# Four pairwise additions in an index lookup, and a denser schedule of gathered rows in the expert stage

## The chip, the cores and the metric

The kernel runs on one core of one Trainium2 chip. The metric is the time of one execution on the device, in microseconds (us). The times below are medians of several executions; the profile is one more execution, recorded by the hardware profiler.

## What is computed

Two layers of a backbone over 256 latent tokens and 256 context tokens, both of width 1024. Each layer has a token mixer (attention, Fourier mixing, pooling, gates) and then an expert network that the reference calls PEER. The change lies in PEER:

```python
def _peer(h, w_pq, peer_keys, peer_down, peer_up):
    q = (h @ w_pq).reshape(B, L, PEER_HEADS, 2, PEER_QDIM // 2)
    s = jnp.einsum("blhpd,hpkd->blhpk", q, peer_keys)
    sv, si = lax.top_k(s, PEER_TOPK)
    cand = (sv[..., 0, :, None] + sv[..., 1, None, :]).reshape(B, L, PEER_HEADS, PEER_TOPK * PEER_TOPK)
    cidx = (si[..., 0, :, None] * N_KEYS + si[..., 1, None, :]).reshape(...)
    top_s, pos = lax.top_k(cand, PEER_TOPK)
    eidx = jnp.take_along_axis(cidx, pos, axis=-1)
    gate = jax.nn.softmax(top_s, axis=-1)
    ...
        a = jnp.einsum("tkd,td->tk", peer_down[ee], hh)
        act = (gg * jax.nn.gelu(a)).astype(hh.dtype)
        return jnp.einsum("tk,tkd->td", act, peer_up[ee])
```

There are 8 heads, 128 keys, 16 picks per head, and so 128 experts for each token out of 16384. The context tokens go through PEER in layer 0 alone; layer 1 has only the 256 latent tokens.

## The kernel before

**Two ways through PEER.** For most tokens the kernel computes all 16384 experts densely: 128 groups of 128 experts, each group multiplied with the weights on TensorE, and the result multiplied by a dense table of gates, G, that is zero where an expert was not picked. In layer 0 this covers 384 of 512 tokens (`ND`). The other 128 tokens (`NS`), one per partition, are done by gathers: for each of the 128 picks GpSimd (POOL) gathers one row of 1024 numbers per token from `down`, VectorE (DVE) forms its dot product with the token's input (L706), and later POOL gathers the row of `up` and DVE adds it, scaled, to an accumulator (L713). That makes 256 such steps, each with one gather of 512 KB; the text calls them *rows*. `rows` is a generator of 256 steps and an end. It keeps two gathers ahead and has three buffers, `gx`. DVE and POOL take their instructions in program order. Each row's DVE instruction is put behind the last weight split that was written before it (`issue_after(self.last)`).

**The expert stage of layer 0** is `experts_both` and `experts`, L767 to L821. Step i of 128 loads the `up` weights of group i, splits them into a high and a low part (ACT writes `wh` at L81, DVE `wl` at L82), does 18 matmuls into `acc` (L789 to L791), and prepares the activations of group i + 4 (`dn`). For the first 60 groups (`EARLY0`) the hidden values were computed earlier, and are loaded from `E` into `ge` (L743); for the others they are computed in the step by 24 more matmuls from `in_downT`. At each step's end `next(pace)` runs the generator of rows at a rate of `ROWS_S` per step for the first 56 steps and `ROWS_N` for the other 72. Every sixth step also advances the modulation of layer 1 (`extra`, weights `in_wmod`). When the 128 steps are through, the sums are transposed (L817) and added to the state (L820), and then `drain(rows)` in `run` writes all rows that are left. After it come a step of modulation and the norm of the latent tokens for layer 1 (`norm`, L215 to L288), whose result the next projections (`latents`, matmuls L91 to L93) need. The sum of the rows is added to the context tokens' state in `rows_out` (L720, L721).

```python
pace = paced(rows, lambda: ROWS_S if done[0] < E.shape[0] else ROWS_N)
def step(i):
    done[0] = i + 4
    next(pace)
    if i % 6 == 5:
        next(extra, None)
```

Rows are also run before the stage: one after each of 16 weight columns in `front` and some beside the scores.

**The index lookup** is the end of `topk`, L602 to L616. For each pick a one-hot mask over 16 candidates is made in bf16 (L607), multiplied with the key numbers (L612), and summed over the 16 candidates by a reduction that walks the candidates with a stride of 16 elements (L614). Each works on 128x1024 elements, half of the heads and one of two key sets at a time: four passes a call. `topk` is called six times, so there are 24 of each. Two calls are woven into the attention of layer 0's latent tokens (`early_routes`), two are in `routes` of layer 0 and two in `routes` of layer 1, beside the building of the gate table (`gates`, L644 to L670) and the hidden values computed early.

The order on each engine is settled when the kernel is built: a scheduler orders the instructions of the program text by when they become ready, and each engine then keeps that order.

Of the kernel before, what the change touches and what calls it, by code (L numbers as in the profile page):

```python
# [16 lines left out]
OP = mybir.AluOpType  # L17
AX = mybir.AxisListType
# [8 lines left out]
WINDOWS = (2, 4, 8, 16)  # L27
TG = 16
EARLY0, EARLY1 = 60, 88
ROWS_O, ROWS_A, ROWS_S, ROWS_N = 1, 0.5, 0.4, 2.6  # L30
SC0, SC1, R0, R1 = 0.5, 0.5, (0.36, 0.46, 0.34), (0.53, 0.9, 0.66)
FILL = (0, 3, 6)
PARTS = ((1, 3), (2, 5), (4,))
# [6 lines left out]
class Net:  # L40
# [520 lines left out]
    def topk(self, sv, si, out):  # L561
        nc, kp = self.nc, self.k
        ts = kp.tile([128, 8, 16], F32, name="tsc", bufs=1)
        pos = kp.tile([128, 128], U32, name="pos", bufs=1)


        for h4 in range(2):
            cd = self.f2([128, 4, 112])
            ra, rb = sv[:, 8 * h4:8 * h4 + 8:2, :], sv[:, 8 * h4 + 1:8 * h4 + 8:2, :]
            nc.vector.tensor_tensor(cd[:, :, 0:64].rearrange("p h (a b) -> p h a b", a=4),  # L570
                                    ra[:, :, 0:4].unsqueeze(3).to_broadcast([128, 4, 4, 16]),
                                    rb.unsqueeze(2).to_broadcast([128, 4, 4, 16]), op=OP.add)
            nc.vector.tensor_tensor(cd[:, :, 64:112].rearrange("p h (a b) -> p h a b", a=12),
                                    ra[:, :, 4:16].unsqueeze(3).to_broadcast([128, 4, 12, 4]),
                                    rb[:, :, 0:4].unsqueeze(2).to_broadcast([128, 4, 12, 4]), op=OP.add)
            for i in range(4):
                hd = 4 * h4 + i
                scr = self.f1([128, 112])
                yield from self.top16(ts[:, hd, :], pos[:, hd * 16:(hd + 1) * 16], cd[:, i, :], scr)
                yield  # L580

        sb = kp.tile([128, 2, 128, 2], BF, name="sb", bufs=1)
        for d in range(2):
            nc.vector.tensor_copy(sb.rearrange("p w (h a) d -> p w h a d", h=8)[:, :, :, :, d],
                                  si.rearrange("p (h w) a -> p w h a", w=2))
        g = kp.tile([128, 8, 16], F32, name="gate", bufs=1)
        sm = kp.tile([128, 8, 2], F32, name="gsum", bufs=1)
        nc.vector.tensor_sub(g, ts, ts[:, :, 0:1].to_broadcast([128, 8, 16]))
        nc.scalar.activation(g, g, AF.Exp)
        nc.vector.reduce_sum(sm[:, :, 0], g, axis=AX.X)  # L590
        nc.vector.reciprocal(sm[:, :, 1], sm[:, :, 0])
        nc.vector.tensor_mul(g, g, sm[:, :, 1:2].to_broadcast([128, 8, 16]))
        pu = self.f2([128, 4, 128], U32)
        nc.vector.tensor_scalar(pu[:, 0, :], pos, 4, None, op0=OP.logical_shift_right)
        nc.vector.tensor_scalar(pu[:, 1, :], pos, 2, None, op0=OP.logical_shift_right)
        nc.vector.tensor_scalar(pu[:, 2, :], pos, 15, None, op0=OP.bitwise_and)
        nc.vector.tensor_scalar(pu[:, 3, :], pos, 3, None, op0=OP.bitwise_and)
        pb = kp.tile([128, 2, 128], BF, name="pb", bufs=1)
        nc.vector.scalar_tensor_tensor(pb[:, 0, :], pu[:, 1, :], -12.0, pu[:, 0, :], op0=OP.add, op1=OP.max)
        nc.vector.scalar_tensor_tensor(pb[:, 1, :], pu[:, 0, :], 4.0, pu[:, 2, :], op0=OP.is_lt, op1=OP.mult)  # L600
        nc.vector.tensor_tensor(pb[:, 1, :], pb[:, 1, :], pu[:, 3, :], op=OP.max)
        ij = kp.tile([128, 2, 128], F32, name="ij", bufs=1)  # L602
        for w in range(2):
            for h4 in range(2):
                ks = slice(64 * h4, 64 * h4 + 64)
                oh = self.f2([128, 4, 16, 16], BF)
                nc.vector.tensor_tensor(  # L607
                    oh, self.iota16.unsqueeze(1).to_broadcast([128, 4, 16, 16]),
                    pb[:, w, ks].rearrange("p (h k) -> p h k", h=4).unsqueeze(2).to_broadcast([128, 4, 16, 16]),
                    op=OP.is_equal)  # L610
                o4 = oh.rearrange("p h a (k d) -> p (h a) k d", d=2)
                nc.vector.tensor_tensor(o4, o4, sb[:, w, ks, :].unsqueeze(2).to_broadcast([128, 64, 8, 2]), op=OP.mult)  # L612
                yield
                nc.vector.reduce_sum(ij[:, w, ks].rearrange("p (h k) -> p h k", h=4),  # L614
                                     oh.rearrange("p h a k -> p h k a"), axis=AX.X)
                yield  # L616
        out += [ij, g]

# [490 lines left out]
```

## Time and profile before

| | us |
|---|---|
| median of 3 executions | 3106.73 |
| lowest and highest | 3104.70 to 3107.01 |
| profiled execution, its own time | 3093.76 |
| its span, first to last instruction | 3092.0 |
| TensorE busy (PE) | 2896.5 (94%) |
| VectorE busy (DVE) | 2341.6 (76%) |
| ScalarE busy (ACT) | 1443.6 (47%) |
| GpSimd busy (POOL) | 322.3 (10%) |
| mean granted TensorE clock | 0.964 |

The profiled execution lies 0.4% under the median of the timed ones. [...] A row of waits names who waited for whom. A matmul that is queued counts as busy, so a busy PE can still be held up by a little.

### The profile page before, as it was taken

What the parts mean: (1) busy time and instruction counts of PE and PEld (TensorE: products, weight loads), DVE (VectorE), ACT (ScalarE), POOL (GpSimd) and SP (SyncE); (2) the same over time, 40 slices, a digit from 0 to 9 for tenths busy, and PEclk for the clock granted to TensorE, in tenths of its full rate; (3) what the DMA queues carried; (4) which work ended last, traced back from release to release, by engine and by line L of the source; (5) the groups of instructions that cost most, each with busy time, mean ns of one, the idle gap of its engine ahead of it and who ended that gap; (6) DMA issues with size and microseconds to landing.
All of it is one profiled execution on the core that took longest, in us unless ns stands there. A gap on an engine that the chain in (4) does not pass through costs nothing.

```text
span 3092.0 us, 53067 instructions
## 1 busy us (share of the span) xinstructions
PE 2896.5 (94%) x18335; PEld 2597.3 (84%) x18335; DVE 2341.6 (76%) x5278; ACT 1443.6 (47%) x2820; POOL 322.3 (10%) x260
## 2 busy tenths in 40 slices
PE   7999899798999999999999996699999999999998
PEld 5799878798999777799998995589889998788997
DVE  6677779889988566688787887755799886676666
ACT  5565444443444333344433332354545555555554
POOL 0000000121000011134333344000000000000000
PEclk8999999999999999999999997799999999999999
DMA  7574443676666877799898987543657778888664
GB/s 249 171 233 144 139 129 116 213 249 199 199 221 213 289 251 263 248 309 327 314 320 308 319 294 264 177 152 123 186 159 228 242 235 283 296 267 286 203 201 141
DMA packets 413519, 708.36 MB, mean 229 GB/s; under 512 B 38336, under 2 KB 160960, under 8 KB 409152
## 3 DMA queue, kind: packets, MB, share of 16 engines
q1 hardware_dynamic: 376384, 570.73, 56.4%
q0 software_dynamic: 36864, 134.23, 13.2%
q8 instruction: 143, 2.34, 0.3%
q14 instruction: 128, 1.05, 0.1%
HBM read 638.49 MB, written 66.32 MB: 228 GB/s over the span
## 4 chain that ended last, share of the span: by engine, by line
PE 43%; DMA 10%; DVE 7%; issue 3%; POOL 1%; ACT 1%; DVEq 0%; SPq 0%; ACTq 0%; POOLq 0%
PE acc L790 6%; PE mm L91 6%; PE acc L791 6%; PE mm L92 6%; PE acc L789 6%; PE mm L93 6%; DMA gx<-in_up,eidx 3%; DMA ge<-E 3%; DVE wl L82 2%; DMA raw<-in_up 1%; DMA gx<-in_down,eidx 1%; PE acc L662 1%; PE acc L91 1%; PE acc L92 1%; PE acc L93 1%
## 5 line engine op out<-in xcount | busy, mean ns | idle before, releaser
L81 ACT CAST wh<-raw 128x512 fp32r<-128x512 f32 x1604 | 973.7, 618 | 834.1 <-PE mm L93 196.3
L82 DVE TENSOR_TENSOR wl<-raw,wh 128x512 fp32r<-128x512 f32 x1604 | 1079.8, 689 | 278.7 <-ACT wh L81 269.3
L91 PE MATMUL mm<-hH,wh 128*128 128x256 f32 (+1 forms) x2432 | 755.6, 311 | 12.8 <-ACT ge L731 8.0
L92 PE MATMUL mm<-hH,wl 128*128 128x256 f32 (+1 forms) x2432 | 748.9, 308 | 12.5 <-DVE wl L82 12.5
L93 PE MATMUL mm<-hL,wh 128*128 128x256 f32 (+1 forms) x2432 | 746.2, 307 | 0.0
L790 PE MATMUL acc<-wl,f 128*128 128x512 f32 x1280 | 506.6, 396 | 16.8 <-DVE wl L82 15.7
L789 PE MATMUL acc<-wh,f 128*128 128x512 f32 x1280 | 502.9, 393 | 5.0 <-ACT f L754 5.0
L791 PE MATMUL acc<-wh,f 128*128 128x512 f32 x1280 | 502.3, 392 | 0.0
L92 PEld LDWEIGHTS mm<-hH,wl 128*128 128x128 f32 x2432 | 467.2, 192 | 19.5 <-DVE wl L82 15.0
L91 PEld LDWEIGHTS mm<-hH,wh 128*128 128x128 f32 x2432 | 466.8, 192 | 18.9 <-ACT ge L731 9.1
L93 PEld LDWEIGHTS mm<-hL,wh 128*128 128x128 f32 x2432 | 466.2, 192 | 0.1
L790 PEld LDWEIGHTS acc<-wl,f 128*128 128x128 f32 x1280 | 242.1, 189 | 77.4 <-DVE wl L82 30.4
L693 POOL DMA_INDIRECT gx<-in_down,eidx x128 | 169.7, 1326 | 1295.5 <-DVE f L713 566.0
L789 PEld LDWEIGHTS acc<-wh,f 128*128 128x128 f32 x1280 | 242.3, 189 | 53.4 <-ACT f L754 5.3
L791 PEld LDWEIGHTS acc<-wh,f 128*128 128x128 f32 x1280 | 242.0, 189 | 49.9
L752 DVE TENSOR_TENSOR ge<-ge,f 128x256 f32<-128x256 f32 (+1 forms) x384 | 136.5, 380 | 180.5 <-DMA ge<-E 147.9
L754 ACT CAST f<-ge 128x384 fp32r<-128x384 f32 (+1 forms) x256 | 117.1, 459 | 284.3 <-DVE ge L752 278.2
L731 ACT ACTIVATE ge<-mm 128x384 f32<-128x384 f32 (+1 forms) x256 | 112.0, 438 | 222.2 <-PE mm L93 215.3
L91 PE MATMUL acc<-hH,wh 128*128 128x256 f32 x688 | 210.2, 306 | 2.0 <-ACT hH L285 2.0
L713 DVE SCALAR_TENSOR_TENSOR f<-gx,av,f 128x1024 f32<-128x1024 f32 x128 | 164.0, 1282 | 56.8 <-DMA gx<-in_up,eidx 56.4
L706 DVE CUSTOM_DVE_ANT_0 gx<-gx,f 128x1024 f32<-128x1024 f32 x128 | 156.3, 1221 | 60.4 <-DMA gx<-in_down,eidx 60.2
L92 PE MATMUL acc<-hH,wl 128*128 128x256 f32 x688 | 199.2, 290 | 0.9 <-DVE wl L82 0.9
(221 smaller groups left out, 3840.8 us busy)
## 6 DMA issues: line engine op xcount, KB each, us to landing
raw<-in_downT SPq DMA_DIRECT2D x512, 256.0 KB, 4.0
raw<-in_up SPq DMA_DIRECT2D x512, 256.0 KB, 4.3
raw<-in_wmod SPq DMA_DIRECT2D x192, 256.0 KB, 3.8
raw<-in_winc SPq DMA_DIRECT2D x172, 256.0 KB, 3.1
G<-f SPq DMA_DIRECT2D x40, 1024.0 KB, 6.0
f<-G SPq DMA_DIRECT2D x32, 1024.0 KB, 7.2
raw<-in_wpq SPq DMA_DIRECT2D x96, 256.0 KB, 3.4
raw<-in_wo SPq DMA_DIRECT2D x48, 256.0 KB, 2.6
```

The lines of the kernel that those rows point to most:

```text
L81: nc.scalar.copy(H, r)
L82: self.last = nc.vector.tensor_sub(L, r, H.bitcast(F32)).ins
L91: t.matmul(out, lhsT=wH, rhs=xH, start=first, stop=False)
L92: t.matmul(out, lhsT=wL, rhs=xH, start=False, stop=False)
L93: t.matmul(out, lhsT=wH, rhs=xL, start=False, stop=last)
L693: nc.gpsimd.indirect_dma_start(out=r, out_offset=None, in_=self.h["up"][0] if up else self.h["down0"], in_offset=bass.IndirectOffsetOnAxis ...
L706: nc.vector.tensor_tensor_reduce(r, r, hot[:, 0, :], op0=OP.mult, op1=OP.add, scale=1.0, scalar=0.0, accum_out=av[:, k:k + 1])
L713: nc.vector.scalar_tensor_tensor(hot[:, 1, :], r, av[:, k:k + 1], hot[:, 1, :], op0=OP.mult, op1=OP.add)
L752: nc.vector.tensor_mul(y, y, Gg[:, :, c, :])
L789: m(p[t][half], lhsT=aH[:, a], rhs=H[:, 0], start=(i == 0), stop=False)
L790: m(p[t][half], lhsT=aH[:, a], rhs=L[:, 0], start=False, stop=False)
L791: m(p[t][half], lhsT=aL[:, a], rhs=H[:, 0], start=False, stop=(i == 127))
```

## The change

Two edits. The rates of rows in the expert stage of layer 0 go from 0.4 and 2.6 to 0.75 and 2.75 per step. The strided reduction of the lookup becomes four additions: eight candidates to eight, four to four, two to two in place in bf16, and the last two into `ij` in fp32. One of the 16 candidates is not zero, so the sums are exact.

```diff
-ROWS_O, ROWS_A, ROWS_S, ROWS_N = 1, 0.5, 0.4, 2.6
+ROWS_O, ROWS_A, ROWS_S, ROWS_N = 1, 0.5, 0.75, 2.75
...
-                nc.vector.reduce_sum(ij[:, w, ks].rearrange("p (h k) -> p h k", h=4),
-                                     oh.rearrange("p h a k -> p h k a"), axis=AX.X)
+
+                for n in (8, 4, 2):
+                    nc.vector.tensor_tensor(oh[:, :, 0:n], oh[:, :, 0:n], oh[:, :, n:2 * n], op=OP.add)
+                nc.vector.tensor_tensor(ij[:, w, ks].rearrange("p (h k) -> p h k", h=4), oh[:, :, 0], oh[:, :, 1],
+                                        op=OP.add)
```

The lines behind the lookup move down by three in the changed kernel: the dot products of rows are L709 there, the additions of rows L716, the state's update L823.

On DVE, at the end of layer 0's expert stage, stood before (`gx` is a gathered row, `wl` a weight split, `xT` the state, `rs` the norm's statistics):

```order
L713 SCALAR_TENSOR_TENSOR f_3782<-gx,av,f_3782 128x1024
L82 TENSOR_TENSOR wl<-raw,wh 128x512
L706 ISA gx,av<-gx,f_3782 128x1024
L175 MEMSET f_21222 128x512
L820 SCALAR_TENSOR_TENSOR xT<-acc,mods_93,xT 128x128 x24
L713 SCALAR_TENSOR_TENSOR f_3782<-gx,av,f_3782 128x1024
L706 ISA gx,av<-gx,f_3782 128x1024
L713 SCALAR_TENSOR_TENSOR f_3782<-gx,av,f_3782 128x1024
L176 CAST f_21222<-sc_87 128x16x4
```

Rows stand on both sides of the state's update and go on between the steps of the norm. The same place in the changed kernel:

```order
L716 SCALAR_TENSOR_TENSOR f_3782<-gx,av,f_3782 128x1024
L755 TENSOR_TENSOR ge<-ge,f_20432 128x256
L755 TENSOR_TENSOR ge<-ge,f_20434 128x128
L82 TENSOR_TENSOR wl<-raw,wh 128x512
L758 TENSOR_TENSOR f_21064<-ge,f_21063 128x384
L82 TENSOR_TENSOR wl<-raw,wh 128x512 x6
L175 MEMSET f_21270 128x512
L823 SCALAR_TENSOR_TENSOR xT<-acc,mods_93,xT 128x128 x24
L176 CAST f_21270<-sc_87 128x16x4
L175 MEMSET f_21271 128x512
```

The last row (L716, first line) now stands ahead of the last group's activations (L758), and none behind it.

On DVE, in the lookup of layer 1's first 128 tokens, stood before (`f_25959` and the like are the masks, `ij` the summed indices):

```order
L614 TENSOR_REDUCE ij<-f_25915 128x64
L607 TENSOR_TENSOR f_25959<-iota16b,pb 128x1024
L82 TENSOR_TENSOR wl<-raw,wh 128x512
L612 TENSOR_TENSOR f_25959<-f_25959,sb 128x1024
L614 TENSOR_REDUCE ij<-f_25959 128x64
```

Each pass is a mask, a product and a reduction, with weight splits between them. The same place in the changed kernel:

```order
L616 TENSOR_TENSOR f_25963<-f_25963 128x4x128
L607 TENSOR_TENSOR f_26010<-iota16b,pb 128x1024
L616 TENSOR_TENSOR f_25963<-f_25963 128x4x64
L612 TENSOR_TENSOR f_26010<-f_26010,sb 128x1024
L616 TENSOR_TENSOR f_25963<-f_25963 128x4x32
L82 TENSOR_TENSOR wl<-raw,wh 128x512
L617 TENSOR_TENSOR ij<-f_25963 128x64
```

The additions of one pass stand between the mask, the product and the weight splits of the next.

## Rows read from the trace of the kernel before

**Rows 1.** Windows: stretch, us, PE, PEld, DVE, ACT, POOL busy, clock, DMA, GB/s.

```profile
1020.00:1291.00 271.00, 255.26 (x1064) 202.85 (x1065) 170.31 (x347) 104.66 (x195) 29.34 (x23) 0.96 0.77 260
1291.00:1886.00 595.00, 590.86 (x2970) 534.27 (x2968) 476.82 (x794) 232.03 (x446) 229.57 (x186) 1.00 0.90 311
1886.00:1958.00 72.00, 27.54 (x95) 19.56 (x94) 52.87 (x103) 17.33 (x35) 27.59 (x23) 0.57 0.69 232
```

**Rows 2.** Windows of L713 alone (rows of up): DVE busy, count in brackets.

```profile
1020.00:1291.00 271.00, 15.50 (x13) 0.96 0.77 260
1291.00:1886.00 595.00, 118.50 (x93) 1.00 0.90 311
1886.00:1958.00 72.00, 21.09 (x17) 0.57 0.69 232
```

**Rows 3.** Windows of L706 alone (rows of down, two instructions each).

```profile
1020.00:1291.00 271.00, 14.75 (x24) 0.96 0.77 260
1291.00:1886.00 595.00, 113.10 (x184) 1.00 0.90 311
1886.00:1958.00 72.00, 9.85 (x16) 0.57 0.69 232
```

**Rows 4.** Timeline of PE behind the expert stage: start us, us, what, [idle before].

```profile
1889.82 0.66 PE L817 MATMUL acc<-ident,f 128*128 128x128 f32 x4 [0.35 <-ACT f L814]
1904.96 0.80 PE L185 MATMUL acc<-wh,f 128*128 128x512 f32 x1 [14.48 <-DVE f L176]
...
1957.19 0.58 PE L91 MATMUL acc<-hH,wh 128*128 128x256 f32 x1 [0.76 <-ACT hH L285]
```

**Rows 5.** Timeline of DVE, same place.

```profile
1895.07 6.17 DVE L820 SCALAR_TENSOR_TENSOR xT<-acc,mods,xT 128x128 f32<-128x128 f32 x24
...
1904.68 0.22 DVE L176 CAST f<-sc 128x64 fp32r<-128x64 f32 x1
...
1914.11 0.16 DVE L225 TENSOR_SCALAR rs<-mm 128x2 f32<-128x2 f32 x1 [2.08 <-PE mm L221]
...
1915.40 0.69 DVE L82 TENSOR_TENSOR wl<-raw,wh 128x512 fp32r<-128x512 f32 x1
...
1954.56 1.28 DVE L271 TENSOR_TENSOR f<-xT,mm 128x512 f32<-128x512 f32 x2
```

**Rows 6.** Waits of DVE from 1886 to 1958, the longest: us in total, times, longest.

```profile
DVE f L713 <- DMA gx<-in_up,eidx: 9.5, 8, 2.1
```

**Rows 7.** Chain that ended last, from 1067 to 1291, shares by line.

```profile
by line: DMA ge<-E 31.0%; DMA raw<-in_up 13.2%; DVE wl L82 11.5%; PE acc L790 8.0%; PE acc L791 7.2%; PE acc L789 6.9%; DVE f L755 6.7%; issue 5.6%; DVE ge L752 2.8%; DMA f<-G 2.1%; DVE gx L706 1.6%; DVE f L713 1.2%; ACT wh L81 0.8%; DVEq L
```

**Rows 8.** Waits of DVE from 1020 to 1291, the longest.

```profile
DVE ge L752 <- DMA ge<-E: 89.8, 38, 4.7
```

**Rows 9.** Waits of DVE from 1291 to 1886, the two longest.

```profile
DVE gx L706 <- DMA gx<-in_down,eidx: 49.6, 35, 4.3
DVE f L713 <- DMA gx<-in_up,eidx: 47.2, 33, 3.7
```

**Rows 10.** The gathers (L693) from 1291 to 1886, from issue to landing.

```profile
DMA to landing us min/median/max: 4.3/6.3/10.0
```

**Rows 11.** DVE groups over the whole span: busy us, mean ns | idle before.

```profile
L656 DVE TENSOR_TENSOR a<-f,gT 128x1536 bf16<-128x1536 bf16 x160 | 148.7, 961 | 5.8 <-PE acc L662 5.8
L652 DVE TENSOR_TENSOR f<-iotab,ijT 128x1024 bf16<-128x1024 bf16 x160 | 106.9, 693 | 0.0
L614 DVE TENSOR_REDUCE ij<-f 128x64 f32<-128x1024 bf16 x24 | 50.7, 2111 | 0.0
```

**Rows 12.** Waits of PE in layer 1's lookups: 2322 to 2342, then 2430 to 2448.

```profile
PE mm L92 <- DVE wl L82: 2.7, 3, 1.3
...
PE acc L662 <- DVE a L656: 3.8, 1, 3.8
```

**Rows 13.** Windows around the lookups of both layers, columns as in the first group.

```profile
440.00:560.00 120.00, 115.70 (x850) 104.49 (x849) 110.51 (x302) 53.86 (x112) 0.00 (x0) 1.00 0.38 117
2290.00:2350.00 60.00, 50.44 (x405) 49.09 (x404) 59.93 (x220) 27.54 (x53) 0.00 (x0) 0.94 0.53 169
```

## The prediction

> **What bounds the kernel now.** I read the windows by stage first, then the timeline around the dip that they show, then the waits and the chain on both sides of it. The expert stage of layer 0 has three parts [rows 1]. In the first (steps 0 to 55, 1020 to 1291 us) PE is busy 255.3 of 271 us, the DMA engines are busy 0.77 and move 260 GB/s; the chain runs mostly through loads of stored hidden values (`ge<-E`, 31%) and of `up` weights (13.2%) [rows 7]. In the second (steps 56 to 127, to 1886) PE is busy 590.9 of 595 us at full clock: it is the bound. [...] DVE takes its work in order, so the state's update, the norm's small steps and the weight splits all wait behind rows that wait for their gathers [rows 6].
>
> **The rows, counted.** The first part takes 56 x 0.4 = 22 rows, the second 72 x 2.6 = 187, and some 24 are left for the third part; the windows show 25 there [rows 2, 3]. With the new rates the two parts ask for 56 x 0.75 = 42 and 72 x 2.75 = 198, that is 20 and 11 more, 31 in all. That covers the 24, so the rows end some two steps before the stage does. The order of the changed kernel says the same: the last row stands ahead of the last group's activations, and none behind the state's update.
>
> **What the third part is worth.** Without rows, the way from the last expert matmul to the first projection is this. The transposes end near 1890.5 [rows 4]; the state's update, 6.17 us, follows them closely and ends near 1894 instead of 1901. From the cast that feeds PE (1904.68) to the norm's first small step (1914.11) it takes 9.4 us now [rows 5]; kept whole, that puts the small steps at 1904. Between them and the diagonal matrices stand nine weight splits of 0.69 us [rows 5] and some eleven small operations, about 8 us: 1912. Diagonals, broadcast and the first part of the normalization need some 4 us more (the last step, from L271 at 1954.56 to the matmul at 1957.19, takes 2.6 [rows 4, 5]): 1916. The splits come from a chain of loads, casts and matmuls at the lower clock that may hold them, so I take 1920. **Gain: 1957 - 1920 = 37 us**, between 30 (the splits wait some 0.8 us each) and 42.
>
> **What the 20 rows cost in the first part.** Below: nothing, if they fall into the time in which DVE waits for `ge`, 89.8 us in 38 waits [rows 8]; a gain is not to be had from more work here. Above: each lies open on DVE with its 1.25 us (15.50 us for 13 additions, 14.75 us for 12 dot products [rows 2, 3]), 25 us. Between these I go by the chain: rows hold 2.8% of the 224 us from 1067 to 1291 [rows 7], 6.3 us for the 21 or so rows there, 0.3 us each. **Cost: 20 x 0.3 = 6, with a little for the transfers 7 us.** Their bytes: 20 x 0.52 MB = 10.5 MB on top of 271 us x 260 GB/s = 70.5 MB, so 299 GB/s if the time stays. The second part moves 311 GB/s with gathers among it [rows 1], so this fits.
>
> **What the 11 rows cost in the second part.** 14 us of DVE work, against 118 us in which DVE is idle, 97 of them waiting for gathers to land [rows 1, 9]. PE has its weights in time there, and three more rows in twenty steps change that little. **Cost: 2 us**, between 0 and the 14.
>
> **What the additions bring.** From 1024 to 1536 elements a bf16 operation of this kind goes from 693 to 961 ns [rows 11]: 0.52 ns an element and 157 ns fixed. The additions of 512, 256 and 128 elements are then 425, 291 and 224 ns, and the last, 64 elements with an fp32 output, at twice the slope also 224: 1.16 us instead of 2.11 us. If all ran at twice the slope it would be 1.63 us. So each of 24 passes gains 0.95 us (at least 0.48), 23 us of DVE in all. What of this is on the path is bounded by what PE waits: where layer 1's lookups stand, DVE is full (59.93 of 60 us) and PE idle for 9.6 [rows 13]; of that, waits of 2.7 us fall among the first four reductions and one of 3.8 us behind the next three [rows 12]. The first vanish, of the last three passes give back 2, and in layer 0, where PE is busy 115.7 of 120 us around the first eight passes [rows 13], I count 1. **Gain: 5 us**, between 2 and 9.
>
> [...] In this trace four operations pay the fixed 157 ns four times, 0.63 us of the 1.16 [rows 11]. [...]
>
> **The sum.** -37 + 7 + 2 - 5 = -33 us. Against the profiled execution's own 3093.8 us this gives 3060.8; it lies 13 us under the median, so the same sum from the median, 3106.7, gives **3074 us**, with an own range of 3057 (all terms at their good ends) to 3097 (two of the four at their bad ends, not all).
>
> **Rivals.**
>
> *No change: the first part pays for the bytes.* If the first part is bound by what the DMA engines bring at its own 260 GB/s, 10.5 MB cost 40 us instead of 7, and the sum is 0: 3107. For it: the chain is 46% loads there [rows 7]. Against it: DMA is busy only 0.77, and 311 GB/s are moved later [rows 1].
>
> *Slower: the first part pays for bytes and DVE one after the other.* A row's gather delays the `ge` load, DVE then waits for `ge`, and the row's own 1.25 us comes on top since DVE keeps its order: 2.0 + 1.25 us a row, 65 us for 20. The sum is -37 + 65 + 2 - 5 = +25: 3132. It decides from 2.0 us a row, where the 40 us of gains net of the second part are eaten. Against it: none of the longest waits of DVE there is for a gather [rows 8], and a row costs the chain 0.3 us now.
>
> *The gathers don't keep up in the second part.* The new rate asks for a row every 595/198 = 3.0 us. Now it is 595/185 = 3.2 us [rows 2, 3]. With three buffers a row's gather (6.3 us at the median from issue to landing [rows 10]) and its 1.25 us on DVE give a pitch of at least 2.5 us; the room is what DVE's order may add. If the pitch stays at 3.2, DVE waits at gathers while weight splits queue behind it, and 198 rows take 634 us instead of 595, less the two steps' room of some 16: +22 instead of +2, 3094. [...]
>
> *The change doesn't do what it says.* The rows were to lag behind their places so far that some are still left at the stage's end, say six at 2.9 us (72 us for 25 rows [rows 2, 3]): 17 us of the 37 stay, 3091. Against it: the order on DVE is fixed, and it has no row behind the update.
>
> **How the numbers follow.** A difference under 0.2% (6 us) can't be told from no change. Forecast 0.73, bytes 0.11, bytes and DVE 0.07, gathers 0.06, rows left 0.03. Faster are the forecast, the gathers and the rows left, 0.82, less 0.01 for the forecast's far tail: 0.81. Same is 0.12, slower 0.07. The range goes from the forecast's lower end, 3057, to 3104: it takes in the two milder rivals and stops short of the bytes and the slower case, which with the tails hold 0.2.
>
> **What would show it.** Behind the stage, no row (L709, L716) after the state's update; the projections' first matmul about 34 us after the last expert matmul instead of 71. The first part 271 us long before and some 278 after, with waits for `ge` no longer than 95 us in total; the second part 597, PE still full. The new operations L616 and L617 at about 425, 291, 224 and 224 ns, and PE's wait of 2.7 us among layer 1's first lookups gone. Wrong would be a first part longer by 25 us or more, PE's busy share in the second part below 98%, or a wait that takes the place of the drained rows, such as splits that wait for the modulation's weights.

## The result, and the profile after

The changed kernel takes **3054.5 us** at the median of four runs (3049.3 to 3060.4); the kernel before 3105.7 at the median of four (3092.9 to 3107.0). The ratio estimated from these runs is 0.985, with an interval of 0.982 to 0.988: faster by 1.5%, some 46 us, where 33 were predicted. The two medians lie 51 us apart; but beside the later experiments the kernel before had medians of 3095.9 to 3098.4 us (11 to 23 executions each), so the gain is nearer to 46. Applied to the 3106.7 us that the forecast started from, the ratio gives 3060 us; the median itself lies 2.5 us under the low end of the range. The profiled execution of after took 3055.25 us (span 3053.5), that of before 3093.8, so the two traces differ by 38.5 us and not by the whole distance of the medians; the rest stands in no trace.

The windows of after, of the three parts of layer 0's expert stage, answer to [rows 1], columns as there (clock is the granted TensorE clock as a share of full speed, DMA the busy share of the DMA engines, GB/s what they moved). Records of matmuls overlap (the last expert matmuls, L792 to L794 from 1892.81 us, have 0.39 us each and start 0.23 us apart), so PE can count as busy while one is queued.

```profile
1010.00:1283.00 273.00, 254.96 (x1066) 204.90 (x1067) 191.16 (x373) 105.21 (x196) 62.86 (x42) 0.96 0.84 290
1283.00:1895.00 612.00, 598.42 (x2968) 535.16 (x2967) 484.85 (x803) 229.27 (x450) 230.08 (x188) 0.99 0.90 309
1895.00:1926.00 31.00, 22.58 (x98) 19.01 (x96) 20.98 (x64) 14.32 (x29) 0.00 (x0) 0.73 0.33 105
```

The first part is 2 us longer, though its DMA engines now move 290 GB/s instead of 260; the second is 17 us longer, which was not foreseen; the third is 41 us shorter and has no gather (POOL x0). The boundaries here are whole us; in the comparisons below the parts are cut at the starts of instructions, as the table has them (us, from the two traces; the first 272 us, ahead of the table, differ by 1 us):

| stretch | before | after | difference |
|---|---|---|---|
| layer 0's first output projection to the end of its second, with the first lookups in between ("early") | 321.1 | 308.5 | -12.6 |
| routes of layer 0 | 427.9 | 430.8 | +2.9 |
| expert stage, steps 0 to 55 | 270.2 | 272.5 | +2.3 |
| expert stage, steps 56 to 127 | 594.1 | 611.7 | +17.6 |
| last expert matmul to first projection of layer 1 | 71.7 | 29.9 | -41.8 |
| projections and attention of layer 1 | 362.7 | 365.7 | +3.0 |
| layer 1's first mask to its expert stage | 286.6 | 279.9 | -6.7 |
| from there to the end | 485.6 | 483.3 | -2.3 |

Behind the stage, the timeline of PE in after (start us, us, what, [idle before]; against [rows 4]):

```profile
1895.08 2.79 PE L820 MATMUL acc<-ident,f 128*128 128x128 f32 x24
...
1902.17 0.78 PE L185 MATMUL acc<-wh,f 128*128 128x512 f32 x1 [4.30 <-DVE f L176]
...
1907.44 3.83 PE L221 MATMUL mm<-ones,f 128*128 128x1 f32 x18
...
1924.56 0.58 PE L91 MATMUL acc<-hH,wh 128*128 128x256 f32 x1 [0.76 <-ACT hH L285]
```

The timeline of DVE in the same place (against [rows 5]):

```profile
1895.72 6.29 DVE L823 SCALAR_TENSOR_TENSOR xT<-acc,mods,xT 128x128 f32<-128x128 f32 x24 [2.22 <-PE acc L820]
...
1911.31 0.16 DVE L225 TENSOR_SCALAR rs<-mm 128x2 f32<-128x2 f32 x1 [7.41 <-PE mm L221]
...
1917.26 0.69 DVE L82 TENSOR_TENSOR wl<-raw,wh 128x512 fp32r<-128x512 f32 x1 [1.75 <-ACT wh L81]
...
1920.73 2.48 DVE L271 TENSOR_TENSOR f<-xT,mm 128x512 f32<-128x512 f32 x4
```

No row stands in it. Work that was late behind rows is now late behind PE: DVE sits idle for 7.41 us until the norm's sums (L221) are there, and these run at a low granted clock: it is 0.51 from 1902 to 1911 us, behind 4.30 us in which PE stood idle, and 0.73 at the mean of the third part (0.57 before). Of the nine splits among the small steps one waits for its cast, 1.75 us.

In the second part the waits of DVE in after (us in total, times, longest us; against [rows 9]):

```profile
DVE gx L709 <- DMA gx<-in_down,eidx: 61.3, 36, 4.5
DVE f L716 <- DMA gx<-in_up,eidx: 53.5, 35, 3.4
```

They grew from 97 to 115 us, and PE's waits there grew with them. Of before:

```profile
PE acc L790 <- DVE wl L82: 2.7, 3, 2.0
PE mm L186 <- DVE wl L82: 1.4, 1, 1.4
```

and of after, where PE waits for the same weight splits 16 times and for activations twice:

```profile
PE acc L793 <- DVE wl L82: 6.1, 12, 1.9
PE mm L91 <- ACT ge L734: 3.8, 2, 3.2
PE mm L186 <- DVE wl L82: 3.6, 4, 1.2
```

The additions in after, as groups over the span (busy us, mean ns | idle before; they take the place of L614 in [rows 11]):

```profile
L616 DVE TENSOR_TENSOR f<-f 128x512 bf16<-128x512 bf16 x24 | 10.0, 417 | 0.0
L616 DVE TENSOR_TENSOR f<-f 128x256 bf16<-128x256 bf16 x24 | 6.8, 284 | 0.0
L616 DVE TENSOR_TENSOR f<-f 128x128 bf16<-128x128 bf16 x24 | 5.2, 218 | 0.0
L617 DVE TENSOR_TENSOR ij<-f 128x64 f32<-128x64 bf16 x24 | 5.2, 216 | 0.1
```

Together 1.135 us a pass instead of 2.111.

### The profile page after: what moved, and what is told of

It is laid out like the page before. It is cut to its first block, busy times and chain, and to the rows that moved or that the text cites. A ratio compares the mean times of both kernels' runs of the same rounds, so it can differ in the third digit from the quotient of the medians.

```text
span 3053.5 us, 53130 instructions
## 1 busy us (share of the span) xinstructions
PE 2895.9 (95%) x18335; PEld 2599.7 (85%) x18335; DVE 2310.3 (76%) x5350; ACT 1438.3 (47%) x2820; POOL 327.4 (11%) x260
## 4 chain that ended last, share of the span: by engine, by line
PE 56%; DVE 18%; DMA 16%; issue 7%; ACT 2%; POOL 1%; DVEq 0%; SPq 0%; ACTq 0%; POOLq 0%
PE mm L91 7%; PE mm L92 7%; PE mm L93 7%; PE acc L793 5%; PE acc L792 5%; PE acc L794 5%; DVE wl L82 4%; DMA ge<-E 4%; DMA gx<-in_up,eidx 4%; PE acc L91 3%; PE acc L93 3%; PE acc L92 3%; DMA gx<-in_down,eidx 3%; DVE a L659 2%; PE acc L665 2%
## 5 line engine op out<-in xcount | busy, mean ns | idle before, releaser
L792 PE MATMUL acc<-wh,f 128*128 128x512 f32 x1280 | 505.0, 394 | 5.0 <-ACT f L757 5.0
L794 PE MATMUL acc<-wh,f 128*128 128x512 f32 x1280 | 503.8, 394 | 0.0
L696 POOL DMA_INDIRECT gx<-in_down,eidx x128 | 178.2, 1392 | 1225.5 <-DVE f L504 553.4
L792 PEld LDWEIGHTS acc<-wh,f 128*128 128x128 f32 x1280 | 243.3, 190 | 53.6 <-ACT f L757 5.3
L794 PEld LDWEIGHTS acc<-wh,f 128*128 128x128 f32 x1280 | 243.0, 190 | 49.8
L755 DVE TENSOR_TENSOR ge<-ge,f 128x256 f32<-128x256 f32 (+1 forms) x384 | 136.2, 379 | 166.9 <-DMA ge<-E 136.9
L716 DVE SCALAR_TENSOR_TENSOR f<-gx,av,f 128x1024 f32<-128x1024 f32 x128 | 163.8, 1279 | 54.4 <-DMA gx<-in_up,eidx 53.5
L709 DVE CUSTOM_DVE_ANT_0 gx<-gx,f 128x1024 f32<-128x1024 f32 x128 | 156.0, 1219 | 63.4 <-DMA gx<-in_down,eidx 63.4
```

Source lines behind the costliest of these rows:

```text
L696: nc.gpsimd.indirect_dma_start(out=r, out_offset=None, in_=self.h["up"][0] if up else self.h["down0"], in_offset=bass.IndirectOffsetOnAxis ...
L709: nc.vector.tensor_tensor_reduce(r, r, hot[:, 0, :], op0=OP.mult, op1=OP.add, scale=1.0, scalar=0.0, accum_out=av[:, k:k + 1])
L716: nc.vector.scalar_tensor_tensor(hot[:, 1, :], r, av[:, k:k + 1], hot[:, 1, :], op0=OP.mult, op1=OP.add)
L755: nc.vector.tensor_mul(y, y, Gg[:, :, c, :])
L792: m(p[t][half], lhsT=aH[:, a], rhs=H[:, 0], start=(i == 0), stop=False)
L794: m(p[t][half], lhsT=aL[:, a], rhs=H[:, 0], start=False, stop=(i == 127))
```

## The experiments

Three questions were open. Which half of the change gives what? Why did a rate that asks for eleven more rows cost the second part 17 us: because gathers, taken in order, don't keep up, or because of the bytes that they move? And are the additions worth the 5 us of waits that PE shows, or all the time that DVE saves? Each kernel was timed against the kernel before on its own chip; the kernels of one line of the list ran together: the halves and the rates 0.9 and 1.1; the four buffers, their control, the doubled mask and the rate 1.25; the two placements of the additions and the rate 1.0.

**The halves.** Additions alone, the rates as before (against the changed kernel):

```diff
-ROWS_O, ROWS_A, ROWS_S, ROWS_N = 1, 0.5, 0.75, 2.75
+ROWS_O, ROWS_A, ROWS_S, ROWS_N = 1, 0.5, 0.4, 2.6
```

> The four additions with the old rates of rows (0.4 and 2.6). Theory A, the two edits act apart from each other: the additions give what the trace of the change shows around the lookups, about 9 us in the early lookups of layer 0 and 4 to 7 us in those of layer 1, so the time is 13 to 17 us under the kernel before; the first part of the expert stage lasts 271 us, the second 594 us, and the third still has some 25 rows and 72 us. Theory B, the second part's extra 17.6 us in the changed kernel come from the additions' new order and not from the rate: the second part here lasts about 610 us and the time is within 4 us of the kernel before. The prediction's own term for the additions was 5 us, with 9 as its upper end.

Rates alone (against the kernel before):

```diff
-ROWS_O, ROWS_A, ROWS_S, ROWS_N = 1, 0.5, 0.4, 2.6
+ROWS_O, ROWS_A, ROWS_S, ROWS_N = 1, 0.5, 0.75, 2.75
```

> The new rates of rows (0.75 and 2.75) with the old reduction. Theory A: the third part shrinks by about 41 us, the first part grows by 2 us (270 to 273) and the second by about 17 us (594 to 611), so the time is 20 to 24 us under the kernel before, and the lookups keep their old lengths. Theory B: the second part stays at about 595 us and the time is 37 to 40 us under.

The additions alone: 3076.7 us, ratio 0.993 (0.991 to 0.994), some 22 us, more than the 13 to 17 expected. The rates alone: 3071.9, ratio 0.992 (0.990 to 0.994), some 26 us (20 to 24 expected). The product is 0.9845 and the change measured 0.985, so the halves add up. Windows of the additions alone, the "early" stretch and the third part:

```profile
271.00:582.00 311.00, 293.44 (x2112) 267.26 (x2110) 250.61 (x857) 140.64 (x289) 10.87 (x10) 0.97 0.46 149
...
1876.00:1945.00 69.00, 27.31 (x94) 19.04 (x93) 52.08 (x102) 16.59 (x34) 25.63 (x22) 0.57 0.72 244
```

Windows of the rates alone, second and third part:

```profile
1292.00:1903.00 611.00, 596.83 (x2967) 533.40 (x2966) 484.90 (x803) 227.81 (x449) 229.29 (x188) 1.00 0.90 309
1903.00:1933.00 30.00, 21.59 (x95) 17.99 (x93) 19.69 (x61) 14.40 (x30) 0.00 (x0) 0.73 0.36 116
```

The short third part and the long second part both belong to the rates; the shorter "early" stretch belongs to the additions. With the old rates the third part stays at 69 us.

**Other rates.** In each, only the line of the rates differs from the changed kernel; every one leaves no row to the third part.

```diff
-ROWS_O, ROWS_A, ROWS_S, ROWS_N = 1, 0.5, 0.75, 2.75
+ROWS_O, ROWS_A, ROWS_S, ROWS_N = 1, 0.5, 0.9, 2.6
```

> The additions with rates of 0.9 and 2.6: the second part gets back its old rate, and the first takes the rows instead (56 x 0.9 = 50, 72 x 2.6 = 187, with the 23 from before it 260, so none are left over). Theory A, at 2.75 a step the gathers with their three buffers can't keep up and DVE waits for them with weight splits behind: the second part goes back to 594 to 597 us, the first grows by 1 to 3 us over the changed kernel, and the time is 12 to 17 us under the changed kernel (60 under the one before). Theory C, it is the mere presence of a denser or differently aligned row pattern, or the clock: the second part stays above 605 us. A rival on the first part, each row there costs 1 us or more: it grows by 8 us or more.

```diff
-ROWS_O, ROWS_A, ROWS_S, ROWS_N = 1, 0.5, 0.75, 2.75
+ROWS_O, ROWS_A, ROWS_S, ROWS_N = 1, 0.5, 1.1, 2.45
```

> The additions with rates of 1.1 and 2.45: 62 and 176 rows, 261 with the 23. If the first part takes rows at the 0.1 to 0.3 us that the trace of the change shows for each, it lasts 274 to 279 us; the second part 594 us, as the rate is under the old one, or a little less if the old rate already cost something there; the time is then 10 to 18 us under the changed kernel. If the first part has no room left at 1.1 a step (its DMA share would go from 0.84 towards 0.9), it lasts 285 us or more and the time is no better than with 0.9 and 2.6.

```diff
-ROWS_O, ROWS_A, ROWS_S, ROWS_N = 1, 0.5, 0.75, 2.75
+ROWS_O, ROWS_A, ROWS_S, ROWS_N = 1, 0.5, 1.25, 2.3
```

> The additions with rates of 1.25 and 2.3: 70 and 166 rows, 259 with the 23. The second part was 611, 598 and 589 us at 2.75, 2.6 and 2.45; PE's own work in it is some 588 us, so it is expected at 586 to 589 us here. The first part was 272, 277 and 280 us at 0.75, 0.9 and 1.1: 282 to 287 us here if each further row costs 0.3 us or so, above 290 us if the DMA engines are full. So the time is expected within 5 us of that of 1.1 and 2.45.

```diff
-ROWS_O, ROWS_A, ROWS_S, ROWS_N = 1, 0.5, 0.75, 2.75
+ROWS_O, ROWS_A, ROWS_S, ROWS_N = 1, 0.5, 1.0, 2.5
```

> The additions with rates of 1.0 and 2.5: 56 and 180 rows, 259 with the 23. Between 0.9 and 2.6 (3044 us) and 1.1 and 2.45 (3035 us): a first part of 277 to 280 us and a second of 589 to 593 us, a time of 3035 to 3044 us. If instead the time is above both, the difference between those two was one of single executions and not of the rates.

Parts from the traces, in us, and the ratios to the kernel before with their intervals:

| rates | first part | second part | third part | sum | ratio |
|---|---|---|---|---|---|
| 0.4, 2.6 (before) | 270.2 | 594.1 | 71.7 | 936.0 | 1 |
| 0.75, 2.75 (after) | 272.5 | 611.7 | 29.9 | 914.1 | 0.985 (0.982 to 0.988) |
| 0.9, 2.6 | 276.9 | 597.7 | 29.8 | 904.4 | 0.983 (0.981 to 0.984) |
| 1.0, 2.5 | 284.3 | 588.7 | 30.0 | 903.0 | 0.982 (0.980 to 0.984) |
| 1.1, 2.45 | 280.0 | 588.7 | 29.7 | 898.4 | 0.981 (0.979 to 0.983) |
| 1.25, 2.3 | 286.2 | 588.7 | 29.8 | 904.7 | 0.985 (0.984 to 0.987) |

The second part has a floor: 588.7 us, reached by every rate up to 2.5; at 2.6 it is 594 to 601 over six kernels, 598.5 at the mean, and at 2.75 611 in two. The trace of before, 594.1, is the shortest of the six. Windows of both parts at 1.1 and 2.45, the quickest kernel of all (3035.2 us):

```profile
1008.00:1288.00 280.00, 257.62 (x1067) 205.94 (x1066) 212.06 (x401) 103.84 (x194) 90.47 (x61) 0.95 0.90 321
1288.00:1876.00 588.00, 588.00 (x2963) 533.56 (x2962) 464.62 (x773) 239.98 (x448) 212.87 (x169) 1.00 0.89 304
```

PE is busy all 588 us: that is its own time. And the bytes don't tell the second parts apart: 304 GB/s here, 309 in after, 311 in before, with a DMA share of 0.89 to 0.90 in all three. In the first part the price of a row grows. Five traces at the rate 0.4 lie between 266.9 and 270.2, 268.4 at the mean; the 20 more rows at 0.75 cost 3.5 us (271.9 at the mean of two), the 39 more at 1.1 some 12, the 48 more at 1.25 some 18. At 0.9 it is 8 us for 28 rows, 4.4 over after where 1 to 3 were expected. The rate 1.0 doesn't fit in: its 34 more rows cost 16 us, and its first part, 284.3 us, is longer than the 277 to 280 expected and than that of 1.1. It is one trace, and this stays open. The window of the first part at 1.25, with the DMA engines at 0.92:

```profile
1011.00:1297.00 286.00, 259.20 (x1065) 206.52 (x1064) 220.39 (x416) 104.07 (x196) 105.92 (x69) 0.94 0.92 328
```

The rate 1.25 is behind 1.1 by 0.5%, some 14 us, where at most 5 were expected; their profiled executions differ by 9.8 us, and the first part accounts for 6 of these. The rest is spread over stretches that the rates don't touch and stays open. The kernels at 0.9, 1.0 and 1.1 have overlapping intervals.

**Four buffers for the gathers.** All rows as in after, but three gathers ahead instead of two. The fourth buffer's room is taken from two of the 14 buffers of `f2`:

```diff
-        return self.f.tile(shape, dt, name="f2", tag="f2", bufs=14)
+        return self.f.tile(shape, dt, name="f2", tag="f2", bufs=12)
...
-            P = self.f.tile([128, 2, TK], F32, name="gx", tag="gx", bufs=3)
+            P = self.f.tile([128, 2, TK], F32, name="gx", tag="gx", bufs=4)
...
-            r = self.f.tile([128, D], F32, name="gx", tag="gx", bufs=3)
+            r = self.f.tile([128, D], F32, name="gx", tag="gx", bufs=4)
...
-        ahead = [gather(*units[0]), gather(*units[1])]
+        ahead = [gather(*units[i]) for i in range(3)]
...
-            if n < 254:
-                ahead.append(gather(*units[n + 2]))
+            if n < 253:
+                ahead.append(gather(*units[n + 3]))
```

> The changed kernel (0.75 and 2.75) with four buffers for gathered rows instead of three and three gathers ahead instead of two; to make room, the work buffers f2 go from 14 to 12, as in the run beside it. Theory A, the second part's extra 17 us come from DVE waiting in its order for gathers that three buffers let start too late: DVE's waits for gathers in the second part fall from 115 us to under 50, the second part lasts 588 to 597 us, and the time is 12 to 20 us under the run beside it. Theory D, it is the rows' work on DVE (1.25 us each) that delays the weight splits, or the bytes: the second part stays above 605 us and the time is within 5 us of the run beside it.

Its control has the 12 buffers of `f2` alone:

```diff
-        return self.f.tile(shape, dt, name="f2", tag="f2", bufs=14)
+        return self.f.tile(shape, dt, name="f2", tag="f2", bufs=12)
```

> The changed kernel with 12 work buffers f2 instead of 14 and nothing else: the control for the run with four gather buffers. The second part is expected at about 611 us as in the changed kernel; whatever other stage gets longer by the two buffers shows here.

Four buffers: 3061.4 us, ratio 0.988 (0.986 to 0.990). The control: 3082.5, ratio 0.995 (0.993 to 0.997). The room taken from `f2` costs some 30 us over the whole kernel (0.995 against 0.985), so this is no better version; but against the control the fourth buffer is worth 21 us. The control was expected to keep the second part at 611 us and made it 9 us longer, so the comparison that counts is with it. Window and waits of DVE in the second part, control:

```profile
1307.00:1928.00 621.00, 597.55 (x2967) 531.80 (x2966) 484.49 (x804) 226.15 (x450) 224.73 (x188) 1.00 0.88 305
...
DVE gx L709 <- DMA gx<-in_down,eidx: 64.7, 33, 4.5
DVE f L716 <- DMA gx<-in_up,eidx: 54.3, 36, 4.3
...
DVE wl L82 <- ACT wh L81: 1.3, 3, 0.6
```

and with four buffers:

```profile
1314.00:1902.00 588.00, 588.00 (x2964) 533.63 (x2963) 486.18 (x801) 245.39 (x449) 256.92 (x187) 1.00 0.91 320
...
DVE wl L82 <- ACT wh L81: 69.6, 56, 2.7
...
DVE gx L709 <- DMA gx<-in_down,eidx: 10.5, 11, 2.0
DVE f L716 <- DMA gx<-in_up,eidx: 5.4, 6, 1.5
```

The same rows, the same DVE work (484 and 486 us), more bytes a second, and the part is 33 us shorter and at PE's floor. What fell is the wait for the gathers, from 119 to 16 us. DVE is still idle for 102 us, 70 of them waiting for ACT's casts, but now no wait of PE is left. (Outside this part the two traces differ by 10 us the other way, hence the 21 us of the whole.) This settles the second question: the pitch of the gathers was the limit, not their bytes and not DVE's work.

**Where the additions count.** A flag for the form of the sum, set in the first lookups alone (rates 0.4 and 2.6), against the kernel before:

```diff
-    def topk(self, sv, si, out):
+    def topk(self, sv, si, out, tree=False):
...
-                nc.vector.reduce_sum(ij[:, w, ks].rearrange("p (h k) -> p h k", h=4),
-                                     oh.rearrange("p h a k -> p h k a"), axis=AX.X)
+                if tree:
+                    for n in (8, 4, 2):
+                        nc.vector.tensor_tensor(oh[:, :, 0:n], oh[:, :, 0:n], oh[:, :, n:2 * n], op=OP.add)
+                    nc.vector.tensor_tensor(ij[:, w, ks].rearrange("p (h k) -> p h k", h=4), oh[:, :, 0], oh[:, :, 1],
+                                            op=OP.add)
+                else:
+                    nc.vector.reduce_sum(ij[:, w, ks].rearrange("p (h k) -> p h k", h=4),
+                                         oh.rearrange("p h a k -> p h k a"), axis=AX.X)
...
-        yield from self.topk(*S[1], r1)
+        yield from self.topk(*S[1], r1, True)
...
-        yield from self.topk(*S[0], r0)
+        yield from self.topk(*S[0], r0, True)
```

> The additions only in the two early lookups (8 of 24 passes, woven into the attention of layer 0's latent tokens), the old reduction in the others, the old rates. Theory E, DVE's saving is time wherever DVE is the engine that the others wait for, whatever the trace names as waits of PE: from the traces so far the stretch up to the end of layer 0's second output projection lasts 320 to 321 us with the reduction and 308 to 312 with the additions, so 9 to 12 us less time here, and nothing in the later lookups. Theory F, the prediction's sum: 1 us.

The same flag, set in layer 1's lookups alone:

```diff
-        drain(weave(self.topk(*S[0], r0), fill, rates[0]))
+        drain(weave(self.topk(*S[0], r0, tg == 0), fill, rates[0]))
...
-        both = (x for pair in zip_longest(chunks(g0, 2), self.topk(*S[1], r1)) for x in pair)
+        both = (x for pair in zip_longest(chunks(g0, 2), self.topk(*S[1], r1, tg == 0)) for x in pair)
```

> The additions only in the lookups of layer 1 (8 of 24 passes), the old reduction in the others, the old rates. Theory E: the stretch from the first lookup of layer 1 to its expert stage lasts 287 us with the reduction and 278 to 280 with the additions, so 7 to 9 us less time. Theory F, the prediction's sum: 4 us. If this run and the one of the early lookups alone together give what the additions give everywhere (about 22 us), the 8 passes of layer 0's routes give nothing.

First lookups alone: 3085.6 us, ratio 0.996 (0.995 to 0.998), 11 us. Layer 1's alone: 3085.9, ratio 0.997 (0.996 to 0.998), 10 us. Together they are the whole of the additions' gain within the intervals (0.9933 against 0.9928), so the eight passes in layer 0's routes bring next to nothing. The rows show in part why. Windows of before, from the first mask to the end of each set of eight passes: first lookups, routes of layer 0, layer 1:

```profile
459.00:563.00 104.00, 99.65 (x732) 89.79 (x730) 98.78 (x265) 46.49 (x98) 0.00 (x0) 1.00 0.36 112
793.00:907.00 114.00, 111.31 (x881) 107.63 (x880) 110.47 (x224) 53.17 (x98) 0.00 (x0) 0.99 0.66 203
2320.00:2440.00 120.00, 116.34 (x1137) 113.92 (x1136) 119.69 (x245) 69.77 (x133) 0.00 (x0) 1.00 0.75 233
```

The same of kernels with additions there, first lookups alone for the first row:

```profile
457.00:553.00 96.00, 95.65 (x715) 87.47 (x714) 88.76 (x284) 44.62 (x94) 0.00 (x0) 1.00 0.38 121
```

and additions alone for the two others:

```profile
780.00:893.00 113.00, 110.34 (x876) 106.62 (x875) 104.94 (x255) 54.48 (x100) 0.00 (x0) 0.98 0.66 207
2307.00:2420.00 113.00, 112.37 (x1114) 110.91 (x1112) 112.64 (x265) 67.36 (x131) 0.00 (x0) 1.00 0.79 243
```

Eight passes save 7.8 us of DVE. The first set is 8 us shorter and layer 1's 7; PE, idle there for 4.4 and 3.7 us, is idle for 0.4 and 0.6 afterwards. That is half of it; the other half is time in which PE counted as busy, in part matmuls that now stand behind the window's end (732 to 715, 1137 to 1114). In the routes of layer 0 PE idled 2.7 us, DVE's saving turns into idle time of DVE (3.5 us before, 8.1 after), and 1 us is gained. DVE was as busy there as in the first set (110.5 of 114 and 98.8 of 104 us), so its busy share doesn't tell the two apart. What differs is PE's wait: in the routes it is one for the building of the gates, and it stays. Waits of PE in the windows of the routes, before and with the additions alone:

```profile
PE acc L662 <- DVE a L656: 2.7, 2, 2.2
```

```profile
PE acc L665 <- DVE a L659: 2.6, 2, 2.2
```

Behind the first lookups stand the first gathers, which wait for their indices; timeline of POOL in before, then with the additions alone:

```profile
563.66 1.24 POOL L693 DMA_INDIRECT gx<-in_down,eidx  x1 [563.21 <-DVE f L504]
```

```profile
555.89 1.08 POOL L696 DMA_INDIRECT gx<-in_down,eidx  x1 [555.45 <-DVE f L504]
```

They start 7.8 us earlier, though the stretch itself begins only 1.1 us earlier, and the end of the output projection behind them takes 19.4 us instead of 22.9 (19.1 with the first lookups alone). Why those 3.5 us go too is not resolved.

**The mask twice.** Additions alone, and DVE's mask, 677 ns, made a second time in each of the 24 passes:

```diff
-                nc.vector.tensor_tensor(
-                    oh, self.iota16.unsqueeze(1).to_broadcast([128, 4, 16, 16]),
-                    pb[:, w, ks].rearrange("p (h k) -> p h k", h=4).unsqueeze(2).to_broadcast([128, 4, 16, 16]),
-                    op=OP.is_equal)
+                for _ in range(2):
+                    nc.vector.tensor_tensor(
+                        oh, self.iota16.unsqueeze(1).to_broadcast([128, 4, 16, 16]),
+                        pb[:, w, ks].rearrange("p (h k) -> p h k", h=4).unsqueeze(2).to_broadcast([128, 4, 16, 16]),
+                        op=OP.is_equal)
```

> The additions with the old rates, and in each of the 24 passes the mask (L607) is computed twice, which adds some 0.63 to 0.70 us of DVE work to a pass and changes no value. Theory E, in the early lookups of layer 0 and in those of layer 1 each microsecond of DVE work is a microsecond of time, and in the routes of layer 0 none is: about 16 x 0.65 = 10 us come back over the additions alone, 4 to 6 in each of the two places, 0 to 1 in the routes of layer 0. Theory F, the prediction's own, only what the trace names as waits of PE in the lookups is on the path: 2 to 3 us come back.

3089.5 us, ratio 0.998 (0.997 to 0.999): of the 22 us of the additions some 16 are gone (10 to 22 by the two intervals), by 16 us of DVE work (24 x 0.677); 10 were expected. The trace shows less: "early" 315.8 us instead of 311.0, layer 1's stretch 280.3 instead of 277.6, the routes of layer 0 no longer, and the rest of it is shorter, so that the two profiled executions last the same (3071.5 and 3071.7 us; the first is the quickest of its twelve). So the size is the medians', and the place of 7.5 us of it is the trace's; where the rest falls is not shown. DVE work in the lookups costs time, where PE's named waits would let only 2 or 3 us through.

## Why the prediction was right, and where its steps failed

- **The rows, counted: right.** None is left behind the state's update; with the old rates 25 were.
- **The third part: right, a little small.** Predicted -37, measured -41.8 (-38 from the mean of the five traces with the old rates, 66.6 to 71.7 us). In before its rows held the projections up: 17 additions and 8 dot products stood there [rows 2, 3], the last addition started at 1953.4 us, and the first projection came at 1957.19 [rows 4]. In after the first projection comes 29.9 us behind the last expert matmul, not 34. The allowance of 4 us for splits that wait was not needed: one of them waits 1.75 us. What is late next is PE's own chain (L221), at the granted clock of 0.51, not the splits.
- **The first part: right, a little dear.** Predicted +7, measured +2.3 (3.5 over all traces of the two rates). DVE's waits for `ge` gave way, as the step said. Waits of DVE there in after, against [rows 8]:

```profile
DVE ge L755 <- DMA ge<-E: 76.7, 40, 4.2
```

  Both rivals that charged the bytes at 2 us a row fall: 290 GB/s were moved in the same time. That cover is finite: the rates 0.9 to 1.25 show it running out.
- **The second part: wrong.** Predicted +2, measured +17.6 (+17 with the rates alone, +13 from the mean of the six traces at 2.6). The prediction's own sign of being wrong came: PE was busy 598.4 of 612 us, under 98%. The rival of gathers that don't keep up, given 0.06 and priced at +22, is what happened. The step that failed took PE for the bound and the 118 us in which DVE was idle as cover for 14 us more of work. But 97 of them were waits for gathers [rows 9]: DVE was not free there, it stood in order in front of a row that had not landed, with weight splits queued behind. In after, for one, it waits 2.08 us for a gather up to 1880.97, adds the row, and two splits follow at 1882.17, though ACT's last cast ahead of them had ended at 1879.40; PE waits 0.29 us for the first.

  So the time of the part followed the rows' pitch, the time from one row to the next. At PE's floor, 588.7 us for 72 steps, the rate 2.75 asks for a row every 2.97 us; in after the 190 rows that DVE did there, the last one ending at 1886.45, took 3.18 us each, as the 185 of before did (3.21). With four buffers 189 rows, the last ending at 1889.2, took 3.04. With three, PE reaches its floor only at the rate 2.5, a row every 3.27 us. At 2.6, the mean of 598.5 us over the 187 rows asked for is again 3.2 us: the rows held the part up in the kernel before already.

  The count was off too: with 42 rows in the first part and 23 ahead of it, 191 of the 256 are left for the second, not 198, so it did 5 rows more and not 11, and DVE's work there grew by 8 us and not 14. The computed pitch of 2.5 us took the landing at its median alone, while the next gather is issued only when DVE has done the row before, late by whatever stands between: in the second part of after POOL sat idle 325 us ahead of gathers in waits for DVE's rows (166.9 for L709, 158.0 for L716).

  The gather instructions that lasted longer beside DVE work (last section) were not the limit: with four buffers POOL was busy longer over the same rows (256.9 against 224.7 us) and the part was at its floor.
- **The additions: wrong in size.** Predicted -5 (2 to 9), measured -22. The durations were right: 425, 291, 224 and 224 ns foreseen, 417, 284, 218 and 216 found. The step that failed read the worth of DVE's time from the waits of PE that fall beside the reductions [rows 12], and in layer 0 counted 1 us of 4.3 us idle [rows 13]. The first lookups gave 11 us and layer 1's 10, where 1 and some 4 were counted: in these two sets what DVE saves comes off the length, nearly one for one, and PE's named waits are half of that. In layer 1 DVE was the bound (119.7 of 120 us); in the first set PE and DVE were nearly even (99.7 and 98.8 of 104), and that DVE's order held PE up there is argued from the runs and not seen in single waits.
- **The fixed cost of small operations.** The prediction read 157 ns from [rows 11], and the additions show some 150 ns in each (417 ns for 512 elements, 284 for 256). Four operations pay it four times, and they are still about half as long as the reduction: 1.135 us a pass against 2.111. Twice the slope for the fp32 output was an estimate; the weight splits of before, 128x512 in fp32, fit it with 689 ns at the mean, 1.04 ns an element beside 157 ns, and the last addition took 216.
- **The sum.** By the runs the rates gave -26 us, where the three steps said -28. The traces give -22: the second and third part together are 641 us instead of 666 to 668 in the five traces with the old rates, -26 where -35 were said, and the first part +3.5 instead of +7; the other 4 us stand in the medians alone. The additions gave 17 us more than said. So the direction was right by its main step, the third part, and the forecast's 33 us fell 13 short of the ratio's 46 (its 3074 us lies 20 above the median), mainly by the additions. That it missed by no more is partly luck: the second part was some 11 to 15 us too cheap, against the additions. The lower end of the range is a slip of 1 us: the four good ends add up to -51, which is 3056 and not 3057.

## What to carry to other kernels

Idle time of an in-order engine is cover only if the engine waits for nothing that the new work also waits for: split it by releaser before it is spent (here 97 of DVE's 118 idle us were waits for gathers, and 8 us more work made the part 17.6 us longer). Where an engine is busy nearly all of a stretch, the single waits that the trace names on PE don't give the worth of its saved time: two of three such stretches gave back nearly all of it, twice what the waits said, and the third 1 us of 8. A busy share alone did not tell them apart; a run for each place did. And where filler work is spread by rates, set the densest stretch just under the pitch that its buffers allow and give the rest to a stretch with waits of another kind: 1.1 and 2.45 took 3035.2 us where 0.75 and 2.75 took 3054.5 (ratios 0.981 and 0.985, whose intervals just touch).

## What the runs showed of the hardware

The strided sum (a stride of 16 elements in bf16) took 2111 ns for 1024 elements; a contiguous fp32 sum in the same kernel of before is cheap, as its group shows:

```profile
L590 DVE TENSOR_REDUCE gsum<-gate 128x8 f32<-128x128 f32 x6 | 1.7, 286 | 0.0
```

That is 1.9 ns an element against some 1.0, if both pay the additions' 150 ns. Type and stride differ together, so which of them costs the time is not shown. With three gathers ahead instead of two each landed a little later. Landing of the gathers (L696) in the second part, in the control and with four buffers:

```profile
DMA to landing us min/median/max: 4.3/6.4/9.9
```

```profile
DMA to landing us min/median/max: 4.2/7.0/11.0
```

The median landing is a tenth later, while the waits for gathers fall to a seventh.

The gather's own instruction on POOL often lasted longer beside DVE work. In the trace of before, the 41 of 256 during which DVE stood idle took 932 to 939 ns each, and the others 1146 ns at the median and up to 5.3 us; in after it is 932 to 940 ns for 45. The same instructions in the second part, in the control and with four buffers, where DVE is idle less (ns, min/median/max):

```profile
L696 POOL DMA_INDIRECT gx<-in_up,eidx x98: 932/938/1941, 1311.8 to 1912.8; - x98
```

```profile
L696 POOL DMA_INDIRECT gx<-in_up,eidx x98: 932/1432/3397, 1312.6 to 1880.8; - x98
```

Spans on POOL are rough, and no run varied this alone.
